# An SSD layer whose projections and scan stand in a fixed order on TensorE, with its gates kept in DRAM and the input also handed over transposed

## The chip, the cores and the metric

One core of one Trainium2 chip runs the kernel. The metric is the device time of one execution in microseconds, as the median of three runs. Engines are named as in the profile: PE is TensorE (PEld its weight loads), DVE is VectorE, ACT is ScalarE, POOL is GpSimd, and SP is SyncE, whose one queue issues all DMAs.

## What is computed

Two blocks follow each other on x of 1024 tokens by 1024 features, all in float32. The first has an RG-LRU and MLA layer (layer A) and an SSD layer, each closed by a layernorm; the second has two feed-forward networks around a mixing layer. The change touches the SSD layer, the first output product behind it, and the start of layer A. The SSD layer, cut to what matters:

```python
proj = x @ w_in                                   # 1024 x 5152
z, xbc, dt = split(proj, [2048, 2048 + 3072])
xbc = silu(causal_conv(xbc))                      # 4 taps
xs, bm, cm = split(xbc)                           # 32 heads of 64; 4 groups of state 128
dt = softplus(dt + dt_bias); a_dt = -exp(a_log) * dt
cs = cumsum(a_dt, within chunks of 128 tokens)
# each chunk c, each group of 8 heads:
y_diag = ((C @ B.T) * causal * exp(cs_l - cs_s)) @ (xs * dt)
states = B.T @ (xs * dt * exp(cs_last - cs))
prev   = prev * exp(cs_last) + states             # from chunk to chunk
y = y_diag + (C @ prev) * exp(cs) + d_skip * xs
y = y * silu(z); y = y * rsqrt(mean(y * y per group)) * norm_w
out = y @ w_out                                   # 2048 x 1024
```

## The kernel before

The program is written with a tile framework that orders the instructions itself: within what data and buffers allow, each engine gets its list from a scheduler that works through the traced code by priority and by times of its own. `issue_after(i)` and `deferred` add edges of order alone: what is traced inside stands behind instruction i on i's engine (PE for the anchors used here), or, for `deferred`, SP's DMAs stand behind it.

A product keeps float32 by splitting both factors into a high and a low part (`split`, L140 and L141) and adding three matmuls (hi·hi, hi·lo, lo·hi). `wload` brings a 512 KB weight tile (L156) and splits it: ACT writes `whi`, DVE writes `wlo`. A column projection (`proj_fm`, L174) is 48 matmuls of 512 columns into one of two PSUM tiles `pa`; a gate tile (L853 to L855) is 96 matmuls of 256 columns. Small results use four PSUM banks `pb`.

Layer A begins with eight loads of x by token tiles, 64 transposes on PE (L201) and their splits; then `lead` multiplies the first two columns.

`ssd_layer` works through four groups of eight heads. `proj(g)` makes B and C (`bc`) and four input columns, each with `conv4` (two ACT reads of PSUM, L331 and L332, and three DVE passes, L334) and a Silu, and turns the inputs to tokens on PE (`tokens`, L821). `gates(g)` makes silu(z), kept in SBUF. `scan(g)` takes eight chunks in three parts:

- `within(c)`: a 512 KB broadcast load of cs (L877), the subtraction on POOL (L883), min on DVE (L884), Exp on ACT (L885); C·B and a transpose on PE (L879, L880); the mask and the product on DVE (L881, L886); three products with the inputs, one on DVE (L887), two on POOL (L888, L889); eight per-head products on PE (L892) and their sum on DVE (L893).
- `between(c)`: the product with the carried state (L901), the new state (L906), and four DVE passes (L902 to L909).
- `finish(c)`: the gate (L915), a sum of squares (L917), nine one-column DVE instructions for the inverse root (L259 to L269), scaling (L919), four transposes (L922) and the store of y.

The dt column (first of `lead`) goes through a softplus of some thirty DVE passes of 256 columns, whose results are transposed on PE (L797 to L802). The scheduler mixes scan(g) with proj(g + 1) on PE as it sees fit. `ssd_out` fills sixteen weight rows (ACT L959, DVE L960) and makes each token tile in two rounds: ten rows early (L658, beside scan 3) and six later.

Of the kernel before, what the change touches and what calls it, by code (L numbers as in the profile page):

```python
# [15 lines left out]
ALU = mybir.AluOpType  # L16
# [376 lines left out]
def layer_a(K, I, XT, get):  # L393
    nc = K.nc

    for i in range(NT):
        if i % 2 == 0:
# [13 lines left out]
    w_in = kp(I["w_in"])  # L411
# [4 lines left out]
    first = lead(K, [wload(K, w_in[:, :, m * P:(m + 1) * P], NK, P) for m in range(2)], get)  # L416
# [339 lines left out]
def ssd_layer(K, I, XT, get, x1, yd):  # L756
# [49 lines left out]
    def proj(g):  # L806
        bc = K.Q2()
        for j, (c0, cj) in enumerate(((4096 + g * P, 16 + g), (4608 + g * P, 20 + g))):
            if g == 0 and j == 0:
                a = first  # L810
            else:
                a = K.A()
                proj_fm(K, a, wload(K, w_in[:, :, c0:c0 + P], NK, P), get)
            conv4(K, bc[:, j, :], a, "s_conv_w", cj, 24, "s_conv_b", copy=True)
            nc.scalar.activation(bc[:, j, :], bc[:, j, :], AF.Silu)
        xs = [K.P2().rearrange("p a (b c) -> p (a b) c", b=2) for _ in range(2)]

        def tokens(m, f):
            b = K.A()
            for q in range(8):  # L820
                nc.tensor.transpose(b[:, q * P:(q + 1) * P], f[:, q * P:(q + 1) * P], K.ident)  # L821
            for h in range(2):
                nc.scalar.activation(xs[h][:, :, m * P:(m + 1) * P],
                                     b[:, 512 * h:512 * h + 512].rearrange("p (q t) -> p q t", q=4), AF.Copy)

        fs = []
        for m in range(4):
            a = K.A()
            c0 = 2048 + g * 512 + m * P
            proj_fm(K, a, wload(K, w_in[:, :, c0:c0 + P], NK, P), get)  # L830
# [3 lines left out]
            fs.append(f)  # L834
            if m:
                tokens(m - 1, fs[m - 1])
        last = lambda: tokens(3, fs[3])
        return bc, xs, last

    def gates(g, late):  # L840
        sz = [K.Q2().rearrange("p a (b c) -> p (a b) c", b=2) for _ in range(2)]
        for hf in range(2):
            c0 = g * 512 + hf * 256
            w = [wload(K, w_in[:, 4 * k:4 * k + 4, c0:c0 + 256], 4, 256) for k in range(2)]
            for h in range(2):
                a = K.A()
                for q in range(4):
                    o = a[:, q * 256:q * 256 + 256]
                    tk = slice((4 * h + q) * P, (4 * h + q + 1) * P)
                    for k in range(NK):  # L850
                        wh, wl = (w[k // 4][m][:, k % 4, :] for m in range(2))
                        xh, xl = get("h", k)[:, tk], get("l", k)[:, tk]
                        nc.tensor.matmul(o, xh, wh, start=k == 0, stop=False)  # L853
                        nc.tensor.matmul(o, xh, wl, start=False, stop=False)  # L854
                        nc.tensor.matmul(o, xl, wh, start=False, stop=k == NK - 1)  # L855
                if hf + h == 0:
                    late()
                nc.scalar.activation(sz[h][:, :, hf * 256:hf * 256 + 256], a.rearrange("p (q c) -> p q c", q=4), AF.Silu)
        return sz

    def scan(g, bc, xs, sz):
        hv = lambda t: t.rearrange("p (h d) -> p h d", h=8)
        held = {}

        def cols(c):
            k0 = (c % 2) * 128 + (c // 2) * 32 + 8 * g
            return lambda t, n: t[:, k0:k0 + 8].unsqueeze(2).to_broadcast([P, 8, n])

        def within(c):
            per_head = cols(c)  # L870
            Bc, Cc = bc[:, 0, c * P:(c + 1) * P], bc[:, 1, c * P:(c + 1) * P]
            X = xs[c // 4][:, c % 4, :]
            rf = K.R2().rearrange("p a b -> p (a b)")
            xdt, xw, y, cbm, bt = rf[:, 0:512], rf[:, 512:1024], rf[:, 1024:1536], rf[:, 1536:1664], rf[:, 1664:1792]
            m = K.S()
            mv = m.rearrange("p (h l) -> p h l", h=8)
            nc.sync.dma_start(mv, cs_d[8 * g:8 * g + 8, c * P:(c + 1) * P].partition_broadcast(P))  # L877
            b = K.B()
            nc.tensor.matmul(b[:, 0:128], Bc, Cc, start=True, stop=True)  # L879
            nc.tensor.transpose(b[:, 128:256], Bc, K.ident)  # L880
            nc.vector.tensor_tensor(cbm, b[:, 0:128], tri, ALU.mult)  # L881
            nc.scalar.activation(bt, b[:, 128:256], AF.Copy)
            nc.gpsimd.tensor_tensor(mv, mv, per_head(csT, P), ALU.subtract)  # L883
            nc.vector.tensor_scalar(m, m, 0.0, None, ALU.min)  # L884
            nc.scalar.activation(m, m, AF.Exp)  # L885
            nc.vector.tensor_tensor(mv, mv, cbm.unsqueeze(1).to_broadcast([P, 8, P]), ALU.mult)  # L886
            nc.vector.tensor_tensor(hv(xdt), hv(X), per_head(dtT, 64), ALU.mult)  # L887
            nc.gpsimd.tensor_tensor(hv(xw), hv(X), per_head(w2T, 64), ALU.mult)  # L888
            nc.gpsimd.tensor_tensor(hv(y), hv(X), dsk[:, 8 * g:8 * g + 8].unsqueeze(2).to_broadcast([P, 8, 64]), ALU.mult)  # L889
            yo = K.B()  # L890
            for h in range(8):
                nc.tensor.matmul(yo[:, 64 * h:64 * h + 64], mv[:, h, :], xdt[:, 64 * h:64 * h + 64], start=True, stop=True)  # L892
            nc.vector.tensor_tensor(y, yo, y, ALU.add)  # L893
            held[c] = Cc, xdt, xw, y, bt

        def between(c):
            per_head = cols(c)
            Cc, xdt, xw, y, bt = held[c]
            if c:
                yp = K.B()  # L900
                nc.tensor.matmul(yp, Cc, prev, start=True, stop=True)  # L901
                nc.vector.tensor_tensor(hv(xdt), hv(yp), per_head(ecs, 64), ALU.mult)  # L902
                nc.vector.tensor_tensor(y, y, xdt, ALU.add)
            if c < 7:
                st = K.B()
                nc.tensor.matmul(st, bt, xw, start=True, stop=True)  # L906
                if c:
                    nc.vector.tensor_tensor(hv(prev), hv(prev), per_head(cdb, 64), ALU.mult)
                    nc.vector.tensor_tensor(prev, prev, st, ALU.add)  # L909
                else:  # L910
                    nc.vector.tensor_copy(prev, st)

        def finish(c):
            _, xdt, xw, y, _ = held[c]
            nc.vector.tensor_tensor(y, y, sz[c // 4][:, c % 4, :], ALU.mult)  # L915
            t = K.small(2, "yss", bufs=3)
            nc.scalar.activation(xw, y, AF.Square, accum_out=t[:, 0:1])  # L917
            rsqrt_col(K, t[:, 1:2], t[:, 0:1], 1, 1.0 / 512, 1e-6)
            nc.scalar.activation(y, y, AF.Copy, scale=t[:, 1:2])  # L919
            yt = K.B()  # L920
            for q in range(4):
                nc.tensor.transpose(yt[:, q * P:(q + 1) * P], y[:, q * P:(q + 1) * P], K.ident)  # L922
            nc.scalar.activation(xdt, yt, AF.Copy)
            nc.sync.dma_start(yd[4 * g:4 * g + 4, :, c * P:(c + 1) * P].rearrange("m p t -> p m t"),
                              xdt.rearrange("p (m t) -> p m t", m=4))

        within(0)
        within(1)
        between(0)
        for c in range(1, 8):  # L930
            between(c)
            finish(c - 1)
            if c < 7:
                within(c + 1)
        finish(7)

    *ops, late = proj(0)
    ops.append(gates(0, late))
    for g in range(4):
        if g == 3:  # L940
            K.scan3 = anchor(K)
        scan(g, *ops)
        if g < 2:
            *ops, late = proj(g + 1)
            ops.append(gates(g + 1, late))
        elif g == 2:
            *ops, late = proj(3)
            ops.append(gates(3, late))


def ssd_out(K, I, yd, x1, x2, ops):

    nc = K.nc
    w_out = I["s_w_out"]
    zd = K.DR([T, D])

    def wsplit(h, l, st, k):
# [59 lines left out]
    for i in range(NT):  # L1017
        if i % 2 == 0:
            zt = K.P2()
# [865 lines left out]
```

## Time and profile before

| | us |
|---|---|
| median of three runs (3438.95 to 3444.36) | 3439.39 |
| the profiled execution's own time | 3432.02 |
| its span | 3430.2 |
| PE busy in the span | 3134.3 (91%) |
| DVE, ACT, POOL busy | 2283.8, 1623.5, 740.0 |

The SSD layer and the early output tiles take the stretch from 558.9 us (the end of `lead` in `ssd_layer`) to 1384.9 us (the end of the eighth early tile). The profile has one execution; matmuls overlap in it, so a piece of PE work is best measured from its start to the start of the next one.

### The profile page before, as it was taken

The page shows a single profiled execution, that of the slowest core. Times are in us where ns is not written, and L with a number is a line of the kernel's source. Part 1 is how long each engine was busy: PE and PEld are TensorE (multiplying, and loading weights), DVE is VectorE, ACT ScalarE, POOL GpSimd, SP SyncE. Part 2 cuts the span into 40 slices and gives each one's busy share as a digit, 9 for nine tenths or more (in the row PEclk, how much of TensorE's full clock was granted, in tenths as well). Part 3 has the DMA queues.
Part 4 walks back from the last instruction along what each step waited for, and adds up shares of the span by engine and source line. Part 5 has one row for each costly group of instructions (what it writes and reads, how often), then busy time and mean ns, then how long its engine had stood idle before and what let it go on. Part 6 is the DMA issues. An engine that isn't in the chain of part 4 may idle for free. (4 is left out here: it accounts for less than half of the span.)

```text
span 3430.2 us, 42421 instructions
## 1 busy us (share of the span) xinstructions
PE 3134.3 (91%) x15624; PEld 2608.4 (76%) x15624; DVE 2283.8 (67%) x3859; ACT 1623.5 (47%) x2951; POOL 740.0 (22%) x455
## 2 busy tenths in 40 slices
PE   8999898989989889879999989899999699999897
PEld 6877776868787767767778877778887588888776
DVE  6537776265656555688775599836666964545998
ACT  5426533344444432364555444553465665554442
POOL 0000011021121211242223354300000333332543
PEclk9999999999999989989999999999999899999999
DMA  3257342122233343423333432345473422223322
GB/s 124 64 200 215 94 150 71 47 64 68 66 70 59 92 157 109 142 71 114 111 118 102 135 117 80 123 147 180 135 186 113 166 68 86 80 86 132 120 80 111
DMA packets 331902, 382.19 MB, mean 111 GB/s; under 512 B 19888, under 2 KB 261680, under 8 KB 331696
## 3 DMA queue, kind: packets, MB, share of 16 engines
q1 hardware_dynamic: 331696, 379.50, 35.4%
q8 instruction: 123, 2.02, 0.2%
q14 instruction: 83, 0.68, 0.1%
HBM read 270.90 MB, written 108.53 MB: 111 GB/s over the span
## 5 line engine op out<-in xcount | busy, mean ns | idle before, releaser
L141 DVE TENSOR_TENSOR wlo<-wst,whi 128x1024 fp32r<-128x1024 f32 (+1 forms) x190 | 227.7, 1202 | 337.7 <-ACT whi L140 337.6
L174 PE MATMUL pa<-x,whi 128*128 128x512 f32 x1568 | 433.0, 397 | 11.6 <-ACT l L332 9.5
L174 PEld LDWEIGHTS pa<-x,whi 128*128 128x128 f32 x1568 | 294.8, 190 | 77.8 <-ACT l L332 10.4
L140 ACT ACTIVATE whi<-wst 128x1024 fp32r<-128x1024 f32 (+1 forms) x190 | 179.9, 948 | 355.9 <-PE pa L174 94.1
L147 ACT ACTIVATE wst<-wst,pk 128x128 f32<-128x128 f32 (+1 forms) x816 | 251.6, 391 | 186.9 <-DMA wst<-in_ffn_w_in_dram 112.6
L174 PE MATMUL pa<-x,wlo 128*128 128x512 f32 x784 | 249.2, 398 | 9.6 <-DVE wlo L141 9.6
L1192 PE MATMUL pb<-x,whi 128*128 128x512 f32 (+1 forms) x736 | 224.1, 381 | 0.0
L1192 PE MATMUL pa<-x,whi 128*128 128x512 f32 (+1 forms) x736 | 221.4, 383 | 2.2 <-DVE p L1028 1.9
L1271 PE MATMUL pa<-wlo,whi 128*128 128x512 f32 x768 | 190.3, 406 | 16.8 <-DVE wlo L141 14.8
L1271 PE MATMUL pb<-wlo,whi 128*128 128x512 f32 x744 | 179.1, 398 | 14.2 <-DVE wlo L141 14.2
L1271 PEld LDWEIGHTS pa<-wlo,whi 128*128 128x128 f32 x768 | 150.5, 197 | 54.0 <-DVE wlo L141 19.2
L174 PEld LDWEIGHTS pa<-x,wlo 128*128 128x128 f32 x784 | 147.9, 190 | 44.6 <-DVE wlo L141 11.5
L1155 POOL TENSOR_TENSOR s<-wst 128x512 f32<-128x512 f32 x44 | 58.5, 1330 | 568.1 <-ACT wst L147 529.3
L1271 PEld LDWEIGHTS pb<-wlo,whi 128*128 128x128 f32 x744 | 142.0, 192 | 47.3 <-DVE wlo L141 17.6
L883 POOL TENSOR_TENSOR s<-s,p 128x1024 f32<-128x1024 f32 x32 | 61.1, 1910 | 538.6 <-DMA s<-d 522.4
L1192 PEld LDWEIGHTS pa<-x,whi 128*128 128x128 f32 x736 | 136.8, 190 | 29.4 <-issue 3.0
L1192 PEld LDWEIGHTS pb<-x,whi 128*128 128x128 f32 x736 | 136.0, 188 | 26.4 <-issue 0.4
L853 PE MATMUL pa<-whi,x 128*128 128x256 f32 x512 | 151.3, 296 | 1.6 <-ACT l L332 1.3
L854 PE MATMUL pa<-wlo,x 128*128 128x256 f32 x512 | 147.4, 288 | 0.0
L855 PE MATMUL pa<-whi,x 128*128 128x256 f32 x512 | 147.2, 288 | 0.0
L140 ACT ACTIVATE whi<-s 128x1024 fp32r<-128x1024 f32 x88 | 93.0, 1057 | 111.9 <-POOL s L1156 59.5
L1192 PE MATMUL pa<-x,wlo 128*128 128x512 f32 (+1 forms) x368 | 141.2, 384 | 4.4 <-DVE wlo L141 4.4
(549 smaller groups left out, 8066.5 us busy)
## 6 DMA issues: line engine op xcount, KB each, us to landing
wst<-in_ffn_w_in_dram SPq DMA_DIRECT2D x88, 512.0 KB, 3.8
d<-p SPq DMA_DIRECT2D x82, 512.0 KB, 3.4
d<-l SPq DMA_DIRECT2D x67, 512.0 KB, 3.8
x<-d SPq DMA_DIRECT2D x128, 256.0 KB, 5.4
p<-d SPq DMA_DIRECT2D x46, 512.0 KB, 4.6
wst<-in_s_w_in_dram SPq DMA_DIRECT2D x40, 512.0 KB, 4.1
s<-d SPq DMA_DIRECT2D x32, 512.0 KB, 9.0
l<-d SPq DMA_DIRECT2D x24, 512.0 KB, 3.9
```

The lines of the kernel that those rows point to most:

```text
L140: K.nc.scalar.activation(hi, src, AF.Copy)
L141: (eng or K.nc.vector).tensor_tensor(lo, src, hi.bitcast(F32), ALU.subtract)
L147: K.nc.scalar.activation(st[:, k, :], st[:, k, :], AF.Copy, scale=col(K, gain, k0 + k))
L174: K.nc.tensor.matmul(ps[:, h:h + 512], w, x[:, h:h + 512], start=k == 0 and m == 0, stop=k == n - 1 and m == 2)
L853: nc.tensor.matmul(o, xh, wh, start=k == 0, stop=False)
L854: nc.tensor.matmul(o, xh, wl, start=False, stop=False)
L855: nc.tensor.matmul(o, xl, wh, start=False, stop=k == NK - 1)
L883: nc.gpsimd.tensor_tensor(mv, mv, per_head(csT, P), ALU.subtract)
L1155: G(s1, a21, a22, ALU.add)
L1192: nc.tensor.matmul(p, l[:, k, :], r[:, k, :], start=k + m == 0, stop=k == 3 and m == 2)
L1271: nc.tensor.matmul(bank[j], th[:, a + o:a + o + P], tw[:, b:b + 512], start=c + m == 0, stop=c == n - 1 and m == 2)
```

## The change

In the SSD layer every piece of work becomes a unit: two state columns, four input columns and four gate tiles in each group. Group g + 1's units alternate with group g's chunks, and each is traced inside `turn()`, which is `issue_after` the last PE instruction traced so far, so the order of PE is that of the code. A chunk n now is: the heads of n, the state step of n, the first part of chunk n + 1, and the end of chunk n - 1. Group 3's chunks alternate with the eight early output tiles. The gates are written to DRAM by each gate tile and read again by the chunk (256 KB) into the buffer of `xw`. The product xs·dt moves from DVE to POOL, and chunks rotate through three buffers instead of two. `ssd_out` becomes a class with three steps; the early tiles take weight rows 8 and 9 first, and these are filled first. In layer A, x comes from a second, transposed copy among the inputs, so the 64 transposes go, and the first two columns are multiplied feature tile by feature tile.

```diff
@@ layer_a
-    for i in range(NT):
-        x = x2[:, i % 2, :]
-        nc.sync.dma_start(x, I["x"][i * P:(i + 1) * P, :])
-        transpose_tokens(K, x, i, XT)
+    first = [wload(K, w_in[:, :, 0:P], NK, P)]
+    for k in range(NK):
+        x = x2[:, k % 2, :]
+        nc.sync.dma_start(x, I["x_fm"][k * P:(k + 1) * P, :])
+        if k == 0:
+            first.append(wload(K, w_in[:, :, P:2 * P], NK, P))
+        split(K, get("h", k), get("l", k), x)
...
+    for k in range(NK):
+        for a, w in zip(heads, first):
+            for h in (0, 512):
+                for m, (l, r) in enumerate(((w[0], "h"), (w[0], "l"), (w[1], "h"))):
+                    nc.tensor.matmul(a[:, h:h + 512], l[:, k, :], get(r, k)[:, h:h + 512],
...
@@ ssd_layer
+    rf = [t.rearrange("p a b -> p (a b)") for t in (K.R2(), K.R2(), K.P2())]
...
+        def gates(hf, h):
...
+            z = K.L()
+            nc.scalar.activation(z, a, AF.Silu)
+            nc.sync.dma_start(sz_d[g][4 * h * P:4 * h * P + 512, hf * 256:hf * 256 + 256].rearrange("(q p) c -> p q c", p=P),
...
+    def within(n):
...
-            nc.vector.tensor_tensor(hv(xdt), hv(X), per_head(dtT, 64), ALU.mult)
+        nc.gpsimd.tensor_tensor(hv(xdt), hv(X), per_head(dtT, 64), ALU.mult)
...
+    def between(n):
...
+        nc.sync.dma_start(xw, sz_d[g][c * P:(c + 1) * P, :])
...
+    def turn():
+        return K.tc.issue_after(anchor(K))
+
+    def chunk(n):
+        with turn():
+            heads(n)
+            between(n)
+            if n % 8 < 7:
+                within(n + 1)
+            if n % 8:
+                finish(n - 1)
+
     for g in range(4):
...
+        for i, unit in enumerate(units(g)):
+            with turn() if g + i else nullcontext():
+                unit()
+            if g and i < 8:
+                chunk(8 * g - 8 + i)
+            if 3 <= i < 7:
+                with turn():
+                    tokens(g, i - 3)
+            if g and i == 8:
+                with turn():
+                    finish(8 * g - 1)
+        with turn():
+            within(8 * g)
+    out.prepare()
+    for i in range(NT):
+        with turn():
+            out.early(i)
+        chunk(24 + i)
+    with turn():
+        finish(31)
```

On PE behind `lead` (pa of 48 matmuls at L174, l the softplus's results, p the table that all chunks read), the kernel before has the transposes of the softplus in the middle of the third column projection:

```order
L174 MATMUL pa608_4553<-x518_3636,whi610_4555 128x512 x2
L174 MATMUL pa608_4553<-x520_3638,whi610_4555 128x512 x2
L797 MATMUL pb591_4405<-ident_99,l586_4341 128x128
L798 MATMUL pb591_4405<-ident_99,l587_4342 128x128
L174 MATMUL pa608_4553<-x518_3636,wlo611_4556 128x512 x2
```

Now the same transposes (L807 to L812) stand directly behind `lead` (L191) and ahead of every column projection:

```order
L191 MATMUL pa_4149<-x_3541,wlo_4144 128x512
L807 MATMUL pb_4310<-ident,l_4246 128x128
L808 MATMUL pb_4310<-ident,l_4247 128x128
L809 MATMUL pb_4311<-ident,l_4247 128x128 x2
L812 MATMUL pb_4311<-p_4132 128x256
L174 MATMUL pa_4338<-x_3540,whi_4340 128x512 x2
```

So two and a half projections that stood ahead of the softplus's transposes now stand behind them. The second place is the third chunk of the first scan, PE again. Before, a chunk's pieces are put into a projection that has already begun:

```order
L174 MATMUL pa731_5754<-x520_3638,whi733_5756 128x512 x2
L892 MATMUL pb665_5301<-r662_5286,s663_5287 128x64 x8
L901 MATMUL pb666_5311<-p577_4227,q593_4418 128x512
L906 MATMUL pb667_5315<-r662_5286 128x512
L922 MATMUL pb670_5333<-ident_99,r652_5229 128x128 x4
L174 MATMUL pa731_5754<-x518_3636,wlo734_5757 128x512 x2
```

Now a whole chunk stands between two whole projections (pa672 and pa686), with the first part of the next chunk (L902, L903) ahead of the end of the last one (L948):

```order
L174 MATMUL pa672_5343<-x503_3541,wlo675_5346 128x512 x2
L916 MATMUL pb678_5406<-p589_4329,s667_5308 128x64 x8
L925 MATMUL pb679_5416<-p563_4132,q590_4330 128x512
L930 MATMUL pb680_5420<-p589_4329 128x512
L902 MATMUL pb682_5430<-q590_4330 128x128
L903 MATMUL pb682_5430<-ident_99,q590_4330 128x128
L948 MATMUL pb685_5453<-ident_99,r588_4328 128x128 x4
L174 MATMUL pa686_5460<-x502_3540,whi688_5462 128x512 x2
```

The heads of a chunk have moved a whole projection behind the first part of that chunk. The third place is DVE between the sums of two chunks' heads (L917) in the same scan, now (rs is the inverse root; s681 is the cs tile of two chunks later; wlo689 belongs to the next projection):

```order
L917 TENSOR_TENSOR r588_4328<-pb664_5289,r588_4328 128x512
L334 SCALAR_TENSOR_TENSOR q649_5136<-raw663_5282,pk_108,q649_5136 128x1023
L909 TENSOR_TENSOR s667_5308<-s667_5308,p589_4329 128x1024
L941 TENSOR_TENSOR r588_4328<-r588_4328 128x512
L899 TENSOR_SCALAR s681_5425<-s681_5425 128x1024
L259 TENSOR_SCALAR rs1684_5442<-yss683_5440 128x1
L269 SCALAR_TENSOR_TENSOR yss683_5440<-rs1684_5442 128x1
L141 TENSOR_TENSOR wlo689_5463<-wst687_5461,whi688_5462 128x1024
L917 TENSOR_TENSOR p589_4329<-pb678_5406,p589_4329 128x512
```

Some rows between are left out there. The product that the heads wait for (L909) now stands ahead of the inverse root, where before the inverse root of an earlier chunk stood directly ahead of L893.

## Rows read from the trace of the kernel before

**Rows 1.** Busy time by stretches: us, PE, PEld, DVE, ACT, POOL, PEclk, DMA share, GB/s.
```profile
558.90:1384.90 826.00, 741.84 (x4075) 623.38 (x4074) 467.87 (x781) 344.74 (x447) 143.01 (x96) 0.93 0.32 82
733.47:737.00 3.53, 3.53 (x17) 3.53 (x17) 3.29 (x10) 2.04 (x3) 0.00 (x0) 0.50 0.02 5
```

**Rows 2.** Waits of PE in 558.9 to 1384.9: total us, times, longest.
```profile
PE pb L922 <- ACT r L919: 13.1, 6, 4.6
PE pb L892 <- DVE rs L260: 11.4, 6, 3.4
```

**Rows 3.** PE in order of time: start us, us, instruction, [idle before].
```profile
618.40 1.20 PE L174 MATMUL pa<-x,whi 128*128 128x512 f32 x4 [1.33 <-ACT l L332]
...
629.42 1.04 PE L821 MATMUL pa<-ident,l 128*128 128x128 f32 x8
631.79 0.39 PE L853 MATMUL pa<-whi,x 128*128 128x256 f32 x1 [1.33 <-ACT l L332]
...
643.41 1.04 PE L821 MATMUL pa<-ident,l 128*128 128x128 f32 x8
...
901.46 1.89 PE L892 MATMUL pb<-r,s 128*128 128x64 f32 x16
903.19 1.08 PE L901 MATMUL pb<-p,q 128*128 128x512 f32 x2
...
905.32 0.70 PE L174 MATMUL pa<-x,wlo 128*128 128x512 f32 x2
...
908.62 0.38 PE L879 MATMUL pb<-q 128*128 128x128 f32 x2
...
908.87 1.17 PE L174 MATMUL pa<-x,whi 128*128 128x512 f32 x4
```

**Rows 4.** DVE in order of time, the softplus from its first pass to its copy.
```profile
557.92 0.29 DVE L239 TENSOR_SCALAR l<-l 128x256 f32<-128x256 f32 x1 [9.36 <-ACT l L777]
...
572.98 1.28 DVE L334 SCALAR_TENSOR_TENSOR q<-raw,pk,q 128x1023 f32<-128x1023 f32 x1 [0.58 <-ACT q L332]
...
583.38 0.69 DVE L800 COPY p<-pb 128x512 f32<-128x512 f32 x1
```

**Rows 5.** Weight rows of the output product: ACT and DVE groups (busy us, mean ns).
```profile
L959 ACT ACTIVATE x<-wst,pk 128x1024 fp32r<-128x1024 f32 x8 | 9.1, 1147 | 25.6 <-DMA wst<-in_s_w_out_dram 16.7 <-PE pa L854 8.9
L960 DVE SCALAR_TENSOR_TENSOR x<-wst,pk,x 128x1024 fp32r<-128x1024 f32 x8 | 10.2, 1280 | 20.4 <-ACT x L959 20.4
```

**Rows 6.** DMA issues, whole span: count, KB each, median us to landing.
```profile
x<-d SPq DMA_DIRECT2D x128, 256.0 KB, 5.4
...
s<-d SPq DMA_DIRECT2D x32, 512.0 KB, 9.0
...
wst<-in_s_w_out_dram SPq DMA_DIRECT2D x16, 512.0 KB, 3.9
```

**Rows 7.** DVE and POOL groups in 558.9 to 1384.9: busy us, mean ns, idle before.
```profile
L887 DVE TENSOR_TENSOR r<-p,p 128x512 f32<-128x512 f32 x32 | 40.5, 1270 | 22.4 <-DMA d<-r 15.2 <-ACT p L823 7.2
L884 DVE TENSOR_SCALAR s<-s 128x1024 f32<-128x1024 f32 x32 | 37.0, 1156 | 127.8 <-POOL s L883 127.8
L264 DVE SCALAR_TENSOR_TENSOR rs<-rs 128x1 f32<-128x1 f32 x96 | 23.4, 244 | 3.0
...
L903 DVE TENSOR_TENSOR r<-r 128x512 f32<-128x512 f32 x28 | 19.2, 685 | 0.1
...
L883 POOL TENSOR_TENSOR s<-s,p 128x1024 f32<-128x1024 f32 x32 | 61.1, 1910 | 538.6 <-DMA s<-d 522.4 <-DVE r L915 14.3 <-ACT s L885 1.9
L889 POOL TENSOR_TENSOR r<-p,p 128x512 f32<-128x512 f32 x32 | 45.9, 1434 | 0.0
```

**Rows 8.** Start of the program: PE in order of time, then a stretch as in rows 1.
```profile
5.43 10.94 PE L201 MATMUL pb<-ident,p 128*128 128x128 f32 x64 [5.43 <-DMA p<-in_x_dram]
...
19.42 0.88 PE L191 MATMUL pa<-x,whi 128*128 128x512 f32 x2 [3.05 <-ACT whi L140]
...
5.00:10.00 5.00, 4.57 (x24) 4.60 (x25) 3.49 (x17) 2.52 (x5) 0.00 (x0) 1.00 1.01 401
```

More of the change, by code (lines that the diff above doesn't have):

```diff
@@ L414, in layer_a @@
     wgv = wg.rearrange("p (a b) -> p a b", a=8)
-    first = lead(K, [wload(K, w_in[:, :, m * P:(m + 1) * P], NK, P) for m in range(2)], get)
+    heads = [K.A() for _ in first]
+    for k in range(NK):
[3 more added lines that the diff above has]
+                    nc.tensor.matmul(a[:, h:h + 512], l[:, k, :], get(r, k)[:, h:h + 512],
+                                     start=k == 0 and m == 0, stop=k == NK - 1 and m == 2)
+    first = heads
     def rnn(m):
@@ L753, in setup, with ssd_layer @@
     nc.sync.dma_start(K.pk, I["pk"])
-def ssd_layer(K, I, XT, get, x1, yd):
+def ssd_layer(K, I, get, yd, out):
     nc = K.nc
@@ L804, in ssd_layer, with column, units, states @@
     nc.scalar.activation(cdb, b2[:, 256:512], AF.Exp)
[L806 to L830, printed above, removed]
+    sz_d = [K.DR([T, 512]) for _ in range(4)]
+    rf = [t.rearrange("p a b -> p (a b)") for t in (K.R2(), K.R2(), K.P2())]
+    hv = lambda t: t.rearrange("p (h d) -> p h d", h=8)
+    groups, held = {}, {}
+    def column(c0):
+        a = K.A()
+        proj_fm(K, a, wload(K, w_in[:, :, c0:c0 + P], NK, P), get)
+        return a
+    def units(g):
+        S = groups[g] = Ctx()
+        S.fs = []
+        def states(j):
+            c0, cj = ((4096 + g * P, 16 + g), (4608 + g * P, 20 + g))[j]
+            if j == 0:
+                S.bc = K.Q2()
+            a = first if (g, j) == (0, 0) else column(c0)
+            conv4(K, S.bc[:, j, :], a, "s_conv_w", cj, 24, "s_conv_b", copy=True)
+            nc.scalar.activation(S.bc[:, j, :], S.bc[:, j, :], AF.Silu)
+        def inputs(m):
+            a = column(2048 + g * 512 + m * P)
             f = K.L()
@@ L833, in proj @@
             nc.scalar.activation(f, f, AF.Silu)
[L834 to L859, printed above, removed]
@@ L937, in ssd_layer @@
-    *ops, late = proj(0)
-    ops.append(gates(0, late))
-    for g in range(4):
[L940 to L957, printed above, removed]
+            S.fs.append(f)
@@ new lines, in units, with tokens @@
+        return ([lambda j=j: states(j) for j in range(2)] + [lambda m=m: inputs(m) for m in range(4)]
+                + [lambda hf=hf, h=h: gates(hf, h) for hf in range(2) for h in range(2)])
+    def tokens(g, m):
+        S = groups[g]
+        if m == 0:
+            mk = K.Q2 if g % 2 else K.P2
+            S.xs = [mk().rearrange("p a (b c) -> p (a b) c", b=2) for _ in range(2)]
+        b = K.A()
+        for q in range(8):
+            nc.tensor.transpose(b[:, q * P:(q + 1) * P], S.fs[m][:, q * P:(q + 1) * P], K.ident)
+        for h in range(2):
+            nc.scalar.activation(S.xs[h][:, :, m * P:(m + 1) * P],
+                                 b[:, 512 * h:512 * h + 512].rearrange("p (q t) -> p q t", q=4), AF.Copy)
@@ L1736, in layout @@
     o["x"] = v["x"][0]
+    o["x_fm"] = v["x"][0].T
     o["pos"] = v["positions"]
```

282 lines of the change are left out of this document (149 added, 133 removed).

## Prediction, on record before the changed kernel ran

> **What bounds the kernel now.** I read the busy times of the whole span first, then the stretch that the change rewrites, then PE's waits in it, then single pieces in order of time. The profile page names PE: 3134.3 of 3430.2 us. In the stretch from the end of the SSD layer's `lead` to the eighth early tile, 826.00 us, PE is busy for 741.84, DVE for 467.87, ACT for 344.74 and POOL for 143.01 [rows 1]. So PE bounds the stretch, no other engine is near it, and 84.2 us are PE's idle time. A part of the 741.84 is slow clock: behind a pause of some 3.5 us the granted clock reads 0.50, the lower of the two levels (1.2 GHz), and 17 matmuls that follow last 3.53 us [rows 1]. The waits are not one wait: the largest two, transposes behind ACT's scaling and heads behind the inverse root, make 13.1 and 11.4 us, up to 4.6 at a time [rows 2]. Both come from an order in which a piece of the scan was issued before its inputs were there.
>
> How much the order can give is what PE's work would last in the stretch at full clock, without a wait. Start to start [rows 3]: a projection 629.42 - 618.40 = 11.02 us for 48 matmuls (0.23 each), a gate tile 643.41 - 631.79 = 11.62, tokens 631.79 - 629.42 less the 1.33 waited = 1.04; a chunk's heads 1.73, heads, carried state, new state and end transposes 905.32 - 901.46 = 3.86, the first part 908.87 - 908.62 = 0.25. There are 23 projections behind `lead` (24 columns, the first by `lead`), 16 gate tiles, 16 tokens, 32 chunks of 4.11 less eight missing state pieces (four chunks have no carried state, four make no new one) of some 0.9 each, and 8 x 60 matmuls in the early tiles. The sum: 253.5 + 185.9 + 16.6 + 124.4 + 110.2 = 690.6, 691 with the softplus's transposes. The stretch holds 826 - 691 = **135 us** beyond that: 84 idle, 51 of slow clock. This is what the new order competes for.
>
> **The change part by part.** The matmuls, weight loads and passes of the stretch stay the same in number; what goes, comes or moves is this.
>
> *The softplus comes to stand ahead of everything.* Its transposes now stand directly behind `lead`; before, two and a half projections stood ahead of them (the order shown). The chain of DVE passes and transposes lasts from 557.92 to 583.38 + 0.69 = 584.07, 26.2 us, with other work in it: the second column's convolution (three passes of 1.28 and 0.58 of waiting, 4.4 us [rows 4]) and two weight splits (2 x 1.28, by the same shape in [rows 5], 2.6). Alone it is some 19 us. Nothing else stands on PE, since the next projection is behind it: 19 us idle. The pause costs clock too; the price of one restart I take from the 17 matmuls, 3.53 - 1.77 = 1.8 us. Together **20.8**. Bounds: 26.2 if the other work stays in the chain, 10 if DVE runs the passes closer together.
>
> *Tokens of group 0.* A token piece waits until ACT has emptied the tile of the convolution before it, 1.33 us [rows 3]. In groups 1 to 3 a whole chunk stands between and covers this; in group 0 there is none: 4 x 1.33 = **5.3**.
>
> *The first early tile.* Rows 8 and 9 of the weights are filled beforehand, but rows 0 to 7 go where the split input was, so their splits wait for the last gate. They pass through two staging buffers: 3.9 us of transfer [rows 6], 1.15 on ACT and 1.28 on DVE [rows 5], so one row in (3.9 + 1.15 + 1.28) / 2 = 3.17 us, against 6 x 0.23 = 1.38 on PE. The first two are staged beforehand: 2.43 + 6 x 3.17 + 1.38 = 22.8 us, where the tile has 13.8 of work. 9 us lost, and 1.8 of clock: **11**. Bounds 8 and 20 (the transfers share the queue with cs and gates).
>
> *Each slot of a unit and a chunk.* A conv slot has 11.02 + 4.11 = 15.1 us of PE. The longest chain that closes on itself runs through the cs tile, which is freed when a chunk's heads have read it: load 9.0 [rows 6], POOL's subtraction 1.91, min 1.16 [rows 7]; behind min on DVE stand the inverse root (three passes of 0.244, six shorter ones: 1.7, at most 9 x 0.244 = 2.2), a weight split of 1.28 and the sum of the next chunk's heads, 0.69, which frees what the end transposes need. The sum is 15.7 to 16.2. The end transposes that depend on it stand one slot and 2 us behind the heads that start it: 17.0 there. So the chain fits by about 1 us, and each of two DVE steps may find a convolution pass of 1.28 ahead of it, which makes it 1.6 to 1.8 too long. I take 1.0 a slot, between these two ends, over the 28 chunk slots in which this chain closes: **28**. Below, nothing; above, 1.8 and a clock restart, say 3 a slot: 84. Waits of 1 us are below the 3.5 us pause that dropped the clock.
>
> *Gates through DRAM.* Sixteen writes of 512 KB and 32 reads of 256 KB. A 256 KB load takes 5.4 us [rows 6]; the read is issued behind the state matmul and DVE needs it in the end of that chunk, one slot later, so about 10 us of cover: nothing. If that cover were gone it would be part of the chain above. The queue SP issues weights some three units ahead, and its share of 0.32 of the DMA time [rows 1] leaves room.
>
> *The product xs·dt goes from DVE to POOL.* It takes 1.27 on DVE, and a like product takes 1.43 on POOL [rows 7]. POOL's work in a chunk becomes 1.91 + 3 x 1.43 = 6.2 us of a 15 us slot, before the mask: covered, nothing. But the rows also show that the two engines get in each other's way: a DVE product of the same 512 columns takes 0.685 elsewhere (L903) and 1.27 at L887 [rows 7], which runs beside POOL. The Trainium skill, "GPSIMD Engine Reference", section "Specifications", states that POOL's SBUF interfaces are shared with VectorE and contended by DVE instructions with two SBUF inputs; by this rule the move relieves no one and the case D below comes out, by the rows alone the time stays as forecast.
>
> Sum of the stretch: 691 + 20.8 + 5.3 + 11 + 28 = **756 us**, a gain of 70.
>
> *The start of layer A.* The 64 transposes, from 5.43 to about 16.4 us, and the wait up to the first product at 19.42 [rows 8] go. The new first matmul needs a weight tile and one feature tile, loaded and split. Transfers run at 401 GB/s there [rows 8], 1.3 us for 512 KB, against 12 matmuls x 0.23 = 2.8 us for each feature tile: PE bounds the rest. I let it start at 9 (the first load's 5.43, a split on ACT and on DVE of about 1.2 each, and a second load): **10 us** gained, 6 if weights and x come late, 12 if they come at once.
>
> Together 80 us: the profiled execution of 3432.0 would become 3352. The median of 3439.4 stands 7.4 above it, so the forecast of the median is **3359**. About 0.2%, 7 us, is what a measurement of this kernel can tell from no change.
>
> **The rivals.**
>
> *B, nothing stalls.* The chain through cs fits in its slot, and the first tile loses 8: 691 + 20.8 + 5.3 + 8 = 725, and 10 at the start: 3328. For it: 1 us of slack in the chain. Against it: the exact places in which convolution passes fall on DVE.
>
> *C, the chain is longer than the slot throughout.* 3 us a slot: 691 + 20.8 + 5.3 + 11 + 84 = 812, a gain of 14 + 10: 3415. For it: in a fixed order every late piece stops all behind it, where before a scheduler had placed whole half projections between; the median of 9.0 for cs hides longer loads, and the gates' transfers are new beside them. [...]
>
> *D, DVE and POOL exclude each other (slower).* Place: the 18 slots with a convolution. DVE's work there: split 1.28, min 1.16, mask 1.27, six passes of 0.685, the small product 0.3, inverse root 1.7, three convolution passes 3.84, together 13.7 us; with POOL's 6.2 in turn 19.9, where PE has 15.1 and on average some 0.7 of tokens. Stall 4.1 x 18 = 74, and with such pauses 1.8 x 18 = 32 of clock; the other 14 slots keep 1.0 each. 691 + 20.8 + 5.3 + 11 + 14 + 106 = 848, less 10 at the start: 12 longer, 3451. It decides from a stall of (836 - 742) / 18 = 5.2 us a conv slot with its clock. For it: 1.27 against 0.685. Against it: a pass that is stretched to 1.27 makes up for 0.6, not for the whole of POOL's 1.43, and DVE and POOL have 468 + 143 = 611 us in 826.
>
> *E, the order does nothing.* DVE's and ACT's chains set the length and only the start's 10 us remain: 3429. For it: waits only change places. Against it: 84 us idle with every other engine under 57% busy.
>
> **How the numbers follow.** Forecast 0.50, B 0.14, C 0.21, D 0.10, E 0.05. The range leaves out D, E and the edges of the forecast's neighbours: 3325 to 3420; the forecast's own is 3335 to 3390 (28 between 0 and 56, the start 6 to 12, the softplus 10 to 26). Faster by over 0.2% takes the forecast, B, C and most of E: 0.87; within 0.2%: 0.04; slower: most of D, 0.09.
>
> **What would show it right or wrong.** Right: PE idle for some 19 us directly behind `lead`, ended by the softplus on DVE; the stretch up to the eighth early tile near 756; pieces of a chunk at a granted clock of 1.00, one run of 4.1 us between two projections; waits at the end transposes of 0 to 2 us; the first early tile waiting for ACT's and DVE's weight splits; layer A's first product near 9 us. Wrong for the forecast: waits of several us at the heads or the end transposes in every slot (C), DVE without gaps while POOL runs, with its products longer than 1.27 (D), or idle time in the stretch still near 84 us (E).

## The result, and the profile after

The changed kernel takes 3382.19 us (median of four runs, 3371.29 to 3385.59) against 3439.17: ratio 0.9827, 95% interval 0.9802 to 0.9852, a gain of 57 us where 80 were forecast. The profiled execution took 3383.42.

First the stretch between the SSD layer's `lead` and the eighth early tile, and its softplus part. Windows of the changed kernel; the columns are us, then busy us of PE, PEld, DVE, ACT and POOL, granted clock, DMA share, GB/s:

```profile
551.80:1342.10 790.30, 711.29 (x4081) 609.40 (x4081) 466.41 (x735) 342.86 (x442) 182.99 (x128) 0.97 0.40 108
551.80:573.00 21.20, 2.72 (x10) 1.59 (x9) 18.70 (x36) 8.02 (x9) 0.00 (x0) 0.60 0.12 32
```

The same for the kernel before, from the end of its `lead` to the last of the 480 early matmuls:

```profile
559.10:1392.00 832.90, 748.74 (x4105) 629.10 (x4105) 467.71 (x780) 345.01 (x448) 143.01 (x96) 0.93 0.32 84
```

[Rows 1] ended this stretch at 1384.90. That was a misreading: the 480th early matmul ends at 1392.0. So the stretch held 833, not 826, and now it is 790. The two windows do not hold quite the same work: in the new order the heads and the carried state of the last chunk and the last two ends, some 3.4 us of PE, stand behind the eighth early tile, in the kernel before ahead of the end of the window. With them the new stretch is 793.5 us, 39 less than before. Another 7 had been gained ahead of it: the `lead` ends at 551.8 instead of 559.1. PE's idle time is 790.30 - 711.29 = 79 us against 84, and most of the gain is clock, 0.97 against 0.93: PE is busy some 34 us less for the same work.

Where PE waits has changed. In the kernel before, the heads (L892) waited for the inverse root; [rows 2] shows one of four such rows (us, times; the last line is from the changed kernel, L916 being its heads):

```profile
  DVE rs L260: 11.4, 6
  DVE rs L259: 10.8, 5
  DVE rs L261: 8.7, 4
  DVE rs L269: 3.1, 2
...
L916 PE MATMUL pb<-r,s 128*128 128x64 f32 x338 | 40.1, 271 | 0.0
```

These 34.0 us are gone: the heads now wait for nothing, and none of their matmuls lasts more than 276 ns, where before some took up to 447. The waits stand at the end transposes instead, as shown below.

PE in order of time, the softplus's transposes behind `lead`; then one row of group 0, and the first early tile:

```profile
568.82 0.45 PE L807 MATMUL pb<-ident,l 128*128 128x128 f32 x1 [16.98 <-DVE l L250]
...
572.96 2.27 PE L174 MATMUL pa<-x,whi 128*128 128x512 f32 x4
...
613.58 1.21 PE L174 MATMUL pa<-x,whi 128*128 128x512 f32 x4 [1.33 <-ACT l L332]
...
1174.48 0.27 PE L903 MATMUL pb<-ident,q 128*128 128x128 f32 x1
1179.57 1.22 PE L668 MATMUL pa<-whi,l 128*128 128x512 f32 x2 [4.82 <-ACT l L140]
...
1192.39 1.19 PE L668 MATMUL pa<-x,q 128*128 128x512 f32 x4 [0.48 <-DVE x L1006]
1194.76 0.73 PE L668 MATMUL pa<-x,q 128*128 128x512 f32 x2 [1.18 <-ACT x L1005]
...
1199.48 1.90 PE L916 MATMUL pb<-r,s 128*128 128x64 f32 x16
```

These answer to [rows 3, 4]. From the end of `lead` to the next projection pass 21.2 us; the first early tile takes 1199.48 - (1174.48 + 0.27) = 24.7 us for 13.8 of work, its clock halved behind the 4.82 us pause. That pause is not for weights: ACT's split L140 of l is that of the tile's own rows of y, whose read SP issues only when the last gate tile is ending (SP, then ACT):

```profile
1173.86 0.89 SPq L681 DMA_DIRECT2D l<-d  x2
...
1179.10 0.73 ACT L140 ACTIVATE l<-l 128x256 fp32r<-128x256 f32 x2 [1.43 <-DMA l<-d]
```

The weight splits (L1005, L1006) cost four shorter waits, 2.8 us together.

The end transposes (L948), their waits in PE's groups of the stretch (busy us, mean ns, idle before and its enders); they answer to [rows 2]:

```profile
L948 PE MATMUL pb<-ident,r 128*128 128x128 f32 x80 | 13.5, 295 | 29.7 <-DVE r L917 13.1 <-DVE p L917 8.5 <-ACT r L945 8.0
L948 PE MATMUL pb<-ident,p 128*128 128x128 f32 x40 | 6.3, 280 | 17.2 <-DVE r L917 10.3 <-ACT p L945 6.9
```

That is 46.9 us. For 31.9 of them the last to come was DVE's sum of the heads (L917), which frees the PSUM bank that the end transposes write. What DVE waits for from 573 on (us, times, longest), and the DMA issues of 690 to 1140 us (count, KB, median us to landing), to be read beside [rows 6]:

```profile
DVE s L899 <- POOL s L898: 52.7, 10, 10.2
DVE r L941 <- DMA r<-d: 49.1, 15, 8.2
DVE p L941 <- DMA p<-d: 27.5, 7, 8.8
```

```profile
s<-d SPq DMA_DIRECT2D x23, 512.0 KB, 9.7
...
r<-d SPq DMA_DIRECT2D x16, 256.0 KB, 9.3
d<-r SPq DMA_DIRECT2D x15, 256.0 KB, 6.7
p<-d SPq DMA_DIRECT2D x8, 256.0 KB, 10.1
```

Two things come late on DVE: the cs tile (s) and the gates read back (r and p, L936, used at L941). The gates land after 9.3 to 10.1 us where 5.4 were expected, and DVE waits 76.6 us for them. One case, in order of time (SP issues the cs load and the gates' read right behind it):

```profile
965.29 0.50 SPq L897 DMA_DIRECT2D s<-d  x1
965.88 1.11 SPq L936 DMA_DIRECT2D p<-d  x1
977.10 1.90 POOL L898 TENSOR_TENSOR s<-s,p 128x1024 f32<-128x1024 f32 x1 [16.41 <-DMA s<-d]
977.57 1.97 DVE L941 TENSOR_TENSOR p<-p 128x512 f32<-128x512 f32 x1 [8.82 <-DMA p<-d]
```

The start, PE in order of time:

```profile
32.48 0.39 PE L424 MATMUL pa<-x,wlo 128*128 128x512 f32 x1
39.17 6.05 PE L440 MATMUL pb<-p,r 128*128 128x512 f32 x8 [6.30 <-issue]
44.66 1.48 PE L174 MATMUL pa<-x,whi 128*128 128x512 f32 x4
```

The first product starts at 7.83. The first two columns end at 32.9, 10.6 us earlier than before, but the gate products L440 then wait 6.30 us and run at half clock. The third column starts at 44.66, before at 47.27.

### The profile page after: what moved, and what is told of

Same layout as the page of the kernel before. It is cut to its first block, busy times and chain, and to the rows that moved or that the text cites. A ratio compares the mean times of both kernels' runs of the same rounds, so it can differ in the third digit from the quotient of the medians.

```text
span 3381.6 us, 42341 instructions
## 1 busy us (share of the span) xinstructions
PE 3093.0 (91%) x15560; PEld 2582.5 (76%) x15560; DVE 2281.6 (67%) x3819; ACT 1623.7 (48%) x2943; POOL 779.2 (23%) x487
## 5 line engine op out<-in xcount | busy, mean ns | idle before, releaser
L174 PE MATMUL pa<-x,whi 128*128 128x512 f32 x1568 | 430.5, 396 | 5.2 <-ACT l L332 2.7
L140 ACT ACTIVATE whi<-wst 128x1024 fp32r<-128x1024 f32 (+1 forms) x190 | 180.0, 949 | 355.9 <-PE pa L174 94.0
L174 PEld LDWEIGHTS pa<-x,whi 128*128 128x128 f32 x1568 | 294.3, 189 | 69.8 <-issue 3.4
L174 PE MATMUL pa<-x,wlo 128*128 128x512 f32 x784 | 244.1, 393 | 1.8 <-DVE wlo L141 1.8
L1309 PE MATMUL pb<-wlo,whi 128*128 128x512 f32 x744 | 180.1, 400 | 13.8 <-DVE wlo L141 13.8
L174 PEld LDWEIGHTS pa<-x,wlo 128*128 128x128 f32 x784 | 148.0, 189 | 34.0 <-DVE wlo L141 2.2
L140 ACT ACTIVATE whi<-s 128x1024 fp32r<-128x1024 f32 x88 | 93.1, 1058 | 108.2 <-POOL s L1194 53.1
```

The costliest lines, as they stand in the source:

```text
L140: K.nc.scalar.activation(hi, src, AF.Copy)
L174: K.nc.tensor.matmul(ps[:, h:h + 512], w, x[:, h:h + 512], start=k == 0 and m == 0, stop=k == n - 1 and m == 2)
L1309: nc.tensor.matmul(bank[j], th[:, a + o:a + o + P], tw[:, b:b + 512], start=c + m == 0, stop=c == n - 1 and m == 2)
```

## The experiments

Ratios are to the kernel before, run beside each kernel on the same chip; its median was 3432.6 to 3439.2 in the four sets of runs, so a difference of two medians and one of two ratios need not agree, and where it matters both are given. The stretch is that of the windows above, measured in each kernel's own trace. In the kernels with the new order it lacks the last chunk's 3.4 us; add them before comparing with the old order (before, e5, e9, e10, e12).

| | median us | ratio, 95% | stretch us |
|---|---|---|---|
| before | 3439.17 | 1 | 833 |
| changed | 3382.19 | 0.9827 (0.9802 to 0.9852) | 790 |
| e1 softplus later | 3364.20 | 0.9798 (0.9784 to 0.9813) | 773 |
| e2 cs in rows of 4 KB | 3340.50 | 0.9728 (0.9713 to 0.9742) | 744 |
| e3 end first | 3431.08 | 0.9993 (0.9983 to 1.0003) | 846 |
| e4 no edges | 3374.16 | 0.9822 (0.9807 to 0.9837) | 784 |
| e5 before, with e2's rows | 3338.68 | 0.9723 (0.9710 to 0.9736) | 735 |
| e6 xs·dt on DVE | 3399.02 | 0.9899 (0.9885 to 0.9912) | 806 |
| e7 e2 and e4 | 3307.19 | 0.9631 (0.9618 to 0.9645) | 721 |
| e8 e1, e2, new order in layer A | 3324.77 | 0.9685 (0.9672 to 0.9698) | 726 |
| e9 before, xs·dt on POOL | 3442.24 | 1.0022 (1.0011 to 1.0034) | 836 |
| e10 before, new start | 3425.42 | 0.9966 (0.9953 to 0.9979) | 833 |
| e11 e2, each load twice | 3340.00 | 0.9721 (0.9705 to 0.9737) | 745 |
| e12 before with e2's rows, e9, e10 | 3335.27 | 0.9710 (0.9690 to 0.9730) | 741 |

**e1.** The tables' transposes (L807 to L814) go into a function that is called behind the third unit of group 0.

```diff
+            if (g, i) == (0, 2):
+                with turn():
+                    tables()
```

> The softplus's transposes and the tables made from them are traced behind the third unit of group 0 instead of ahead of all units, all else as in the changed kernel. Theory A (the 17 us pause behind the lead is the softplus's chain with nothing else allowed on PE): the pause goes, with its clock, 19 to 22 us less than the changed kernel's 3382, about 3361. Rival (the weight loads or the convolutions that the softplus delays on DVE are late anyway): the pause breaks up into waits of the next projections, less than 8 us gained, about 3376.

The stretch falls by 17.5 us (772.8), and the pause is gone. On the whole it is 18 us by the medians and 10 by the ratios (the kernel before was 6.5 us lower beside it). Theory A holds in kind, 1.5 us below its range in the stretch.

**e2.** The cs table is laid out by chunk, so that eight heads of a chunk stand together.

```diff
-    cs_d = K.DR([32, T])
+    cs_d = K.DR([8, 32, P])
...
-        nc.sync.dma_start(mv, cs_d[8 * g:8 * g + 8, c * P:(c + 1) * P].partition_broadcast(P))
+        nc.sync.dma_start(m, cs_d[c, 8 * g:8 * g + 8].rearrange("h l -> (h l)").partition_broadcast(P))
```

> The cs table lies in DRAM by chunk, so that a chunk's 512 KB broadcast load reads rows of 4 KB instead of 512 bytes; nothing else differs. Theory A (the end transposes wait because this load holds the min, and with it the sum of the heads behind it, on DVE): the load takes 4 to 6 us instead of 9.9, the waits at the end transposes fall from 47 us to under 15, and the time by 35 to 60 us, to 3325 to 3345. Rival B (they wait because their PSUM bank is the one that the same chunk's sum of heads frees, whatever the load takes): the waits stay above 35 us, the time within 10 of 3382. Rival C (contention of DVE and POOL sets the chain): as B, with DVE's products at the same mean length.

Theory A's numbers come: 46 us off the stretch, 34 (ratios) to 42 (medians) off the whole. The waits at the end transposes fall to 13.4 us. The DMA issues of 690 to 1100 us:

```profile
s<-d SPq DMA_DIRECT2D x22, 512.0 KB, 5.0
...
r<-d SPq DMA_DIRECT2D x15, 256.0 KB, 4.5
d<-r SPq DMA_DIRECT2D x14, 256.0 KB, 2.5
```

Every transfer beside the cs load got shorter too, so e2 alone doesn't say whether the late cs tile or the slow neighbours cost the time. e11 does.

**e11.** e2, with each broadcast load issued a second time into the same buffer.

```diff
+        for _ in range(2):
+            nc.sync.dma_start(m, cs_d[c, 8 * g:8 * g + 8].rearrange("h l -> (h l)").partition_broadcast(P))
```

> The changed kernel with the cs table by chunk, each broadcast load of a chunk issued twice in a row into the same buffer (the second brings the same values). Theory A (what costs is how late the cs tile is there): 10 us instead of 5 until both have landed, as in the changed kernel; the waits at the end transposes go back to 35 to 50 us, the time to within 12 us of the changed kernel. Rival (what costs is the 512-byte rows, which slow the other transfers): the waits stay under 20, within 10 us of the rows of 4 KB alone.

Theory A fell. The second load starts when the first has landed, so the tile is there some 9 us after the first issue (median 9.1, against 9.9 in the changed kernel), and DVE's wait for it is longer than there (one pair of loads and the subtraction behind it; DVE's wait, 573 to 1300 us; then the DMA issues, 690 to 1100 us):

```profile
758.71 0.46 SPq L899 DMA_DIRECT2D s<-d  x1
763.65 0.32 SPq L899 DMA_DIRECT2D s<-d  x1
767.61 2.75 POOL L900 TENSOR_TENSOR s<-s,p 128x1024 f32<-128x1024 f32 x1 [6.81 <-DMA s<-d]
```

```profile
DVE s L901 <- POOL s L900: 65.6, 23, 8.9
```

```profile
s<-d SPq DMA_DIRECT2D x45, 512.0 KB, 4.6
...
r<-d SPq DMA_DIRECT2D x16, 256.0 KB, 4.9
d<-r SPq DMA_DIRECT2D x14, 256.0 KB, 4.4
```

Still the end transposes wait 15.6 us in all and the time is e2's. More bytes are moved, the gates stay at 4.9 us. So a late cs tile by itself costs next to nothing here. What separates it from e2 and e11 is the load of 512-byte rows and the slow transfers beside it; DVE's wait for the gates is 76.6 us there and 15.6 here. That the gates are the transfer that counts is read from these rows and not shown: no run moved their read alone, and none has late gates with an early cs tile.

**e3.** The end of chunk n - 1 is traced ahead of the heads of n.

```diff
         with turn():
+            if n % 8:
+                finish(n - 1)
             heads(n)
...
-            if n % 8:
-                finish(n - 1)
```

> The end of chunk n - 1 is traced ahead of the heads of chunk n instead of behind the first part of chunk n + 1; the same instructions. Rival B (the bank): the end transposes no longer ask for the bank that the same chunk's heads free, the waits of 47 us fall under 15, 3325 to 3345. Theory A (DVE in order behind a late cs load): the end's own inverse root now has to be done one piece earlier, the wait stands ahead of the heads in place of behind them, 3370 to 3400.

Both expectations missed: the whole gain is lost. The end transposes now wait for ACT's scaling alone (L948's waits, us and times):

```profile
  ACT r L945: 41.1, 16
  ACT p L945: 26.7, 9
```

The waits grew from 46.9 to 67.8 us and lengthened, and the granted clock of the stretch fell to 0.92. So the bank is not a cause by itself: it hands on what DVE waits for, and with it out of the way the end waits for its own inverse root instead. One place in a chunk's order is worth 56 us of the stretch.

**e4.** `turn()` returns an empty context, so no edge ties PE to the code's order.

```diff
     def turn():
-        return K.tc.issue_after(anchor(K))
+        return nullcontext()
```

> The code of the changed kernel in its order, but without the edges that tie PE to it: the scheduler lets the end transposes slip some 2 us into the projection behind them, and the softplus's transposes behind the third projection; gates through DRAM, the xs product on POOL and the three buffers stay. Theory A (each late piece is paid because nothing may pass it): softplus 20 and most of the end transposes' 70 with their clock come back, 40 to 80 us, 3300 to 3340. Rival D (the chain around the cs tile has a longer period than the slot): the waits appear at the heads instead, only the softplus's 20 come back, about 3362. Rival E (the fixed order is what gained, and without it PE goes back to the old waits): 3390 to 3430.

Within the intervals this is the changed kernel: none of the three expectations. The softplus's 17 us of idle time are gone and the end transposes wait 17.4 us instead of 46.9, but projections, gate tiles and early tiles wait more instead, and PE is busy 721.65 us instead of 711.29 at a clock of 0.95: the stretch is only 7 us shorter. With the slow load, the edges neither earn nor cost much.

**e5.** The kernel before with e2's edit.

> The kernel before with the cs table by chunk, so that its 32 broadcast loads read rows of 4 KB; nothing else. Theory A2 (this load held back only the new order, in which the end of a chunk stands right behind the first part of the next): within 10 us of the kernel before. Rival (the old order waits for the same load; 127.8 us of DVE's idle time stood ahead of its min): 25 to 50 us less, the order's own gain stays as it was; then the load is a fault of both kernels, and the order is worth 40 us with either.

The largest surprise: 96 us, more than the whole change, so both expectations missed. And the order's own gain does not stay as it was: with the short load, the kernel before (0.9723) and the changed kernel (e2, 0.9728) are the same. DVE's idle time ahead of min was 127.8 us in [rows 7], the largest of DVE's there, and it shrinks with the load (groups of DVE in the stretch):

```profile
L885 DVE TENSOR_SCALAR s<-s 128x1024 f32<-128x1024 f32 x32 | 31.9, 999 | 29.2 <-POOL s L884 29.2
```

With it the heads' waits for the inverse root fall from 34.0 to 10.4 us, and those of the end transposes from 13.1 to 0.2. Both kernels were held back by the same 32 loads, the old order by 98 us of its stretch and the new one by 46. There are no gates in DRAM in the old order; whether there the late tile or the transfers beside it cost the time stays open, as no run loads twice in it.

**e6** and **e9.** The xs product back on DVE in the changed kernel, and on POOL in the kernel before:

```diff
-        nc.gpsimd.tensor_tensor(hv(xdt), hv(X), per_head(dtT, 64), ALU.mult)
+        nc.vector.tensor_tensor(hv(xdt), hv(X), per_head(dtT, 64), ALU.mult)
```

> The changed kernel with the xs product on DVE again, as before the change. Theory A (the move costs nothing and gives nothing, since DVE has room and waits for the cs load): within 8 us of the changed kernel. Rival D (DVE and POOL get in each other's way, so POOL's share is paid by DVE): 10 to 25 us faster. Rival F (DVE's order is the tight one): 10 to 25 us slower, the waits at the end transposes above 55 us.

> The kernel before with the xs product on POOL, nothing else. Theory G (DVE's list is what the heads and the end transposes wait for, in both orders, so 1.27 us off it in each chunk is worth what it was in the changed kernel, where taking it back cost about 25 us): 10 to 30 us less than the kernel before. Rival (it pays only in the new order, where the product would stand ahead of the sum of the heads): within 8 us.

In the new order the move is worth 0.7% (15 us of the stretch, 17 to 25 on the whole), by waits at the end transposes of 53.5 against 46.9 us and more clock lost: rival F in kind. In the old order it is worth nothing, rather 0.2% less. Theory G fell: what an engine's relief pays depends on the order.

**e7.** e2 and e4 together.

> The cs table by chunk, and no edges that tie PE to the code's order. Theory A (with a short load the end transposes are in time in the fixed order, so the edges' one price is the softplus): 8 to 17 us faster than with the rows of 4 KB alone, softplus waits shorter, no L948 of its own. Rival E (the edges keep PE's pieces together and are worth something once the load is short): 5 to 20 us slower than with the rows of 4 KB alone.

Better than either theory: 33 us faster than e2 and the fastest kernel of the study. The stretch of e2, then of e7 (columns as in the windows above):

```profile
553.50:1297.50 744.00, 701.42 (x4081) 603.10 (x4081) 477.09 (x735) 340.67 (x442) 186.72 (x128) 0.98 0.38 115
```

```profile
551.20:1271.80 720.60, 700.81 (x4082) 602.08 (x4080) 478.18 (x735) 344.17 (x444) 198.89 (x128) 0.99 0.38 118
```

No end transpose waits any more, and the 17 us pause of the softplus is gone, as its transposes stand behind a later projection. With short loads the edges cost 23 us of stretch: these 17 and the 13.4 at the ends, less some waits that are new at gate tiles.

**e8.** e1, e2, and in layer A the last four feature tiles first for column one, then for column two.

```diff
+    steps = [(k, j) for k in range(4) for j in range(2)] + [(k, j) for j in range(2) for k in range(4, NK)]
```

> Three edits together: the cs table by chunk; the softplus's transposes behind the third unit; and in layer A's first two columns the last four feature tiles first for column one, then for column two, so that column one's convolution lies beside column two's matmuls. Theory A: the first two add, 34 + 10 by the runs' medians (46 + 17 in the stretch up to the eighth early tile); and the 6.3 us pause ahead of layer A's gate products goes, with 2.4 us of clock: the third column starts at 38 instead of 44 to 46. In all 48 to 62 us less than the changed kernel, ratio to before about 0.967. Rival (the time is given back later, as part of the start's gain was): 30 to 45 us, third column at 42 or later.

49 (ratios) to 57 us (medians) less than the changed kernel, and e2's and e1's gains add in the stretch (744 - 18 = 726). The third edit missed: the pause in layer A is 4.90 us instead of 6.30, and the third column starts at 42.9, because DVE's passes of another table (L307) stand between those of the convolution.

**e10.** The kernel before with the changed kernel's `layer_a`.

> The kernel before with the changed kernel's layer A alone (x handed over transposed, first two columns by feature tile). Theory: the third column starts 1 to 3 us earlier, since of the 10.6 us by which the first two columns end earlier 6.3 are waited for the first column's convolution and 2.4 go to the clock; 0 to 5 us on the median. Rival (the other 4 to 8 us, which show between the attention stage's start and the SSD layer in the changed kernel's traces, belong to the start too): 6 to 11 us.

Both are partly right. The third column starts 1.5 us earlier, as the theory has it; the whole is 10 to 12 us (0.34%) faster, as the rival has it. The rest appears in the attention stage, PE and clock in 258 to 411 us, before and e10:

```profile
258.00:411.00 153.00, 134.92 (x814) 119.65 (x814) 108.06 (x236) 87.74 (x202) 0.00 (x0) 0.93 0.57 166
```

```profile
258.00:411.00 153.00, 140.87 (x871) 124.78 (x871) 113.74 (x253) 93.12 (x216) 0.00 (x0) 0.96 0.57 165
```

In the same 153 us more work is done, at a higher clock, though that stage's code is the same. At 397 us of the trace of before, e10 is 8.2 us ahead and the changed kernel 9.6, while with the old start e5 is 3.4 behind and e9 2.1 ahead, so some us of it are scatter between executions. Why was not settled.

**e12.** Rows of 4 KB, xs·dt on POOL and the new start in the kernel before.

> The kernel before with the cs table by chunk, the xs product on POOL and the new start: everything that single runs found to pay, without the new order and without gates through DRAM. Theory H (the new order earned its time only by making the slow load cost less): 3300 to 3315, within 10 us of the changed kernel's best form without edges (0.963). Rival I (alternating whole units with chunks is worth something by itself): above 3322, ratio above 0.968.

Rival I holds: 0.971 against e7's 0.963, 27 us; of the 20 by which the stretches differ, 3.4 are the last chunk. The alternating units, traced in that order, with gates in DRAM, three buffers and the early tiles' own order of rows, are worth this much once the load is short and the edges are off; no run takes these apart. Against e5, the start and the xs product count as they did in e10 and e9: 0.9723 - 0.0034 + 0.0022 = 0.9711.

## Why the prediction was right or wrong

**Range and sign** held: 3382 lies in 3325 to 3420. The gain was 57 of 80 us by the medians; the two profiled executions differ by 49, about midway between the forecast's 80 and rival C's 24. And it came in another way than the sum has it. The terms leave 61 us of idle time (19, 5.3, 9 and 28), 23 less than before, and 4 of slow clock, 47 less. Measured are 79 us idle, 5 less, and some 34 less of slow clock. So the sign that was set for E, idle time near 84 us, came while the time fell.

**Terms that came out.** The softplus, 20.8 forecast, is 21.2 in the trace (18.5 idle, the rest the transposes at a clock of 0.60), and e1 gives 17.5 back. Group 0's tokens, 5.3 forecast, are three waits of 1.33.

**A term that came out by luck.** The first early tile, 11 forecast, loses 24.7 - 13.8 = 10.9. But the weight splits, 9 in the sum, cost 2.8; 4.82 are the wait for the tile's rows of y, which the sum does not have, and the rest is clock.

**The term that was mis-sized** is "each slot of a unit and a chunk", 28 us. What is left of the stretch is 793.5 - 691 - 21 - 4 - 11 = some 66, of which 46.9 are waits at the end transposes in 24 places, up to 5.5 us long, and most of the rest clock. The upper bound of 84, which is rival C's value, held it and is nearer than 28. Waits of about 1 us were taken to be free of clock, as they are shorter than the pause of 3.5. In the changed kernel one of half that length was not free; from 590.2 to 593.4, behind it, the granted clock is 0.50:

```profile
588.57 0.74 PE L174 MATMUL pa<-x,wlo 128*128 128x512 f32 x2 [1.79 <-DVE wlo L141]
589.15 1.10 PE L174 MATMUL pa<-x,whi 128*128 128x512 f32 x4
590.08 1.03 PE L174 MATMUL pa<-x,wlo 128*128 128x512 f32 x2
590.90 1.91 PE L174 MATMUL pa<-x,whi 128*128 128x512 f32 x4
```

The mechanism was wrong as well: "the longest chain that closes on itself runs through the cs tile". e11 makes that tile nearly as late and pays next to nothing. As far as the rows show, the step that failed is **"gates through DRAM … nothing"**: the 5.4 us of [rows 6] is a load's time beside other neighbours. Beside the cs load, issued at the same point of the chunk, it was 9.3 to 10.1. The cover of about 10 us was not always there either: in the case shown DVE was ready 2.9 us after the issue and waited 8.82. Rival C had named this, "the gates' transfers are new beside them".

**"The product xs·dt … covered, nothing"** was wrong in this order: e6 puts it at 0.7% in the change's favour. Case D did not come. By its rule DVE's products beside POOL should be long: in the changed kernel the gate product L941 lasts 1.43 us on average, 0.684 us before (L915), and 1.48 in e6, where the xs product is on DVE. The one shown above, 1.97, stands beside POOL's subtraction; one with no POOL work beside it, at 957.97, takes 0.69. So the two do get in each other's way, in agreement with the Trainium skill ("GPSIMD Engine Reference", section "Specifications"). But not always on DVE's side: in e11 the gate product lasts 0.684 though 14 of the 32 stand beside the subtraction, and it is the subtraction that is longer there, 2.23 against 2.00. It was not the xs product that did it, and moving it to POOL paid.

**The start**, 10 forecast, is 10 to 12 by e10, but not by the steps given: the first product starts at 7.83, where 9 was forecast, but of 10.6 us at the end of the first two columns 1 to 3 are left at the third, where PE now waits for the convolution of column one; the rest comes later, unexplained.

**Errors of sum and reading.** The stretch before was 7 us longer than read, so the forecast of 756 meant a gain of 77; its 691 has all 32 chunks, so 793.5 is the number to hold against it, and the sum of the parts was off by 37 us, all of it in the slots. And "the waits are not one wait" took one row of [rows 2] for the whole: the heads' waits for the inverse root make 34.0 of the 84 us.

**What the sum took for granted** was that the order decides. e4 and e5 say otherwise: without edges nothing changes with the slow load, and the old order with a quick load is 96 us faster. [Rows 7] had the sign, 127.8 us of DVE's idle time behind the cs load; the prediction does not use it, as it takes DVE for an engine far from the bound.

## What to carry to other kernels

Before moving work to get around a late input, ask what makes it late: here one layout of a table, eight rows of 512 bytes instead of one of 4 KB for each partition, took 96 us off the old order, more than the whole change, and 34 to 42 off the new one. A DMA's landing time from a profile holds beside the transfers it stood with: the gates' read, issued right behind the slow load, took that load's 9 to 10 us and not the 5.4 read elsewhere. And edges that fix an order have to earn their place: here dropping them changed nothing with the slow load and gained 33 us with the short one.

## What the runs showed of the hardware

A 512 KB broadcast to 128 partitions in rows of 512 bytes took 9.9 us, in rows of 4 KB 5.1 (medians over the program, changed kernel and e2). The short rows also lie 4 KB apart, the long ones are in one piece; no run separates the length from the distance. The Trainium skill ("DMA: Bandwidth & Descriptors", section "Specifications") puts the least size for full rate at 512 bytes; the measurement here speaks against taking rows of that size as good enough. And the load of short rows slowed what stood beside it: a 256 KB read took 9.3 us beside it and 4.5 beside the long rows, a 256 KB store 6.7 and 2.5, with the same bytes. Twice the loads in the longer rows (e11) hardly slowed the read, 4.9, and the store less, 4.4.
